# Conformer layer: four opening blocks instead of two, part of the convolution's wide sums on GpSimd, one weight group and the moments on TensorE in column groups

## The chip, the cores and the metric

The program runs on one core of one Trainium2 chip. The metric is the device time of one execution in microseconds (us); each kernel is run several times and the median is taken. The engines are called PE (TensorE: matmuls), PEld (its weight loads), DVE (VectorE), ACT (ScalarE), POOL (GpSimd) and SP (SyncE, which here only issues DMA transfers). An engine executes its own queue strictly in order; a transfer or a result of another engine is waited for by a semaphore.

## The reference

A trunk of two layers on 256 positions of width 2048, batch 1, all in float32. Every sublayer is normalised, modulated and gated by vectors computed from a conditioning vector `c` (adaLN):

```python
def causal_dwconv(u, w, b):          # depthwise, K = 31 taps
    ...
def conformer_conv(u, w_pw1, b_pw1, w_dw, b_dw, ln_g, ln_b, w_pw2, b_pw2):
    v = u @ w_pw1 + b_pw1            # 2048 -> 4096
    a, gt = jnp.split(v, 2, axis=-1)
    v = a * jax.nn.sigmoid(gt)       # GLU
    v = causal_dwconv(v, w_dw, b_dw) # 31 taps per channel
    v = jax.nn.silu(layernorm(v, ln_g, ln_b))
    return v @ w_pw2 + b_pw2         # 2048 -> 2048
def sq_relu_mlp(u, w1, w2):
    h = jax.nn.relu(u @ w1)          # 2048 -> 8192
    return (h * h) @ w2
...
mod = silu(c) @ w_mod                # per layer six vectors: shift, scale and gate, for mixer and MLP
x = x + gate * mixer(rmsnorm(x) * (1 + scale) + shift)   # layer 0: conformer, layer 1: Mamba-2
x = x + gate * mlp(rmsnorm(x) * (1 + scale) + shift)
```

The change touches only the Conformer convolution of layer 0 and the computation of `mod` that goes on beside it; the MLPs and the Mamba mixer are left as they are.

## The kernel before

Channels lie on the 128 partitions and the 256 positions in the free dimension, so the width of 2048 is 16 channel tiles ("ct"), held as 4 groups ("g") of 4.

**Product pw1 and its opening.** `native` multiplies by `w_pw1` in plain float32 (L546). The 4096 outputs are 8 blocks; a block takes 4 groups of the input (one 1 MB weight tile each) and yields the value and gate halves of two channel tiles in two PSUM banks. The first `FIRST = 2` blocks are opened together: `before(g)` computes the shift and scale of input group g, `make_u` normalises it (L471 on DVE, L474 on ACT), and both blocks multiply it before the next group is made. The other six blocks follow one by one.

**The vectors.** One job `gemv(layer, seg, ct)` streams 1 MB of `w_mod` and gives 128 numbers. Most jobs are one DVE instruction over 128x2048 with an accumulated sum (L247). The groups in `PE_GROUPS` are computed on PE instead: four matmuls with one column as the stationary side (`scol`) into one row (L236), then a copy and four tiny matmuls that turn the row into columns (L240 to L245). Jobs that nothing waits for soon are queued in `jobs`, and `pump(n)` issues n of them between other work; the `RATE` tables say how many at each step. The transfers go through one queue on SP in program order, into rings of slots called `wm` (2), `hid` (4) and `w` (3).

**The depthwise convolution.** `glu_conv` makes the gated row (L487 on ACT, L488 on DVE) into one of 4 padded rows. For each ct, ACT multiplies 24 of the 31 taps, 256 elements each (L497; 12 for the last two cts), in sets of four; DVE adds the sets as 128x1024 sums (L503), adds the other 7 taps by multiply-add (L506), folds the four partial sums (L508, L510) and subtracts a common row (L517) into the centred row `acc`. ACT squares it (L524), and POOL adds row and square to two running sums (L529, L530).

**The chain to pw2.** After the last ct, PE turns the running sums into columns (L578), DVE and ACT make mean and reciprocal deviation on 128x2 columns (L582 to L588), `spread` turns them back into rows by a diagonal matmul (L432, L433), and each ct is normalised (L596, L597), passed through silu (L598) and split in two parts for the next product (L401, L402). The product pw2 (`outer`, L300) follows; its weights are split by a cast on ACT (L292) and a subtraction on DVE (L293). All later products of the kernel are made in this way.

**Order.** The program is written in one sequence; a scheduler places each engine's instructions by priority as they become ready, `high_priority(n)` moves some ahead, and the order of SP's transfers is kept as written.

Of the kernel before, what the change touches and what calls it, by code (L numbers as in the profile page):

```python
# [8 lines left out]
F32 = mybir.dt.float32  # L9
# [6 lines left out]
P = 128  # L16
# [22 lines left out]


# [17 lines left out]
PE_GROUPS = {(0, SC2, 0), (0, SH2, 0)}  # L58
# [86 lines left out]
class Trunk:  # L145
# [40 lines left out]
    def prologue(self):  # L186
# [12 lines left out]
        for i in range(4):  # L199
# [10 lines left out]
                                compare_op=ALU.is_ge, fill=NEG, base=0, channel_multiplier=-1)  # L210
        self.eps = self.const("eps", [P, 1])
# [10 lines left out]
    def gemv(self, layer, seg, ct):  # L222

        nc = self.nc
        self.ring += 1
        tag = self.rings[self.ring % len(self.rings)]
        w = self.b(tag, [P, D], bufs=4 if tag == "hid" else 2)
        self.stream(w, self.a["wmT"][layer, seg, ct])
        g, i = divmod(ct, 4)
        m = self.mod_tile(layer, seg, g)  # L230
        if (layer, seg, g) in PE_GROUPS:
            if i == 0:
                self.row_sums = self.bank(self.ms, "ms")
            for t in range(4):
                kt = 4 * i + t
                nc.tensor.matmul(self.row_sums[:1, :], lhsT=self.scol[:, kt:kt + 1], rhs=w[:, t * 512:(t + 1) * 512],  # L236
                                 start=kt == 0, stop=kt == NT - 1)
            if i == 3:
                row = self.t("t2", [P, 512], bufs=3)[:1, :]
                nc.scalar.copy(out=row, in_=self.row_sums[:1, :])  # L240
                pc = self.bank(self.ms, "ms")
                for j in range(4):
                    nc.tensor.matmul(pc[:, j:j + 1], lhsT=row[:, j * P:(j + 1) * P], rhs=self.ones[:1, :1],
                                     start=True, stop=True)
                nc.scalar.copy(out=m, in_=pc[:, :4])  # L245
        else:
            nc.vector.scalar_tensor_tensor(out=w, in0=w, scalar=1.0, in1=self.scb, op0=ALU.mult,  # L247
                                           op1=ALU.mult, accum_out=m[:, i:i + 1])
        if i == 3:
            self.mod_done(layer, seg, g)  # L250

    def mod_done(self, layer, seg, kg):
        nc = self.nc
        m = self.mod_tile(layer, seg, kg)
        nc.gpsimd.tensor_tensor(out=m, in0=m, in1=self.col("b_mod", (layer * 6 + seg) * NT + 4 * kg, 4), op=ALU.add)  # L255
        if seg in (SC1, SC2):
            g = "norm_mix_g" if seg == SC1 else "norm_mlp_g"
            nc.gpsimd.tensor_scalar(out=m, in0=m, scalar1=1.0, scalar2=1.0, op0=ALU.add, op1=ALU.mult)
            nc.gpsimd.tensor_tensor(out=m, in0=m, in1=self.col(g, layer * NT + 4 * kg, 4), op=ALU.mult)
# [106 lines left out]
    def outer(self, srcs, make, evac, pump):  # L366

        banks = [[self.bank(self.mm, "mm") for _ in range(2)] for _ in srcs]
        for g in range(4):
            x = make(g)  # L370
            for b, src in enumerate(srcs):
                w = self.load_w(src[g])
                self.pump(pump(g))
# [22 lines left out]
    def split_x(self, dst, t, src, bias=None):  # L396
# [3 lines left out]
        if bias is None:  # L400
            nc.scalar.copy(out=hi, in_=src)  # L401
            nc.vector.tensor_tensor(out=lo, in0=src, in1=hi.bitcast(F32), op=ALU.subtract)  # L402
        else:
            nc.scalar.activation(out=hi, in_=src, func=AF.Identity, bias=bias)
            nc.vector.scalar_tensor_tensor(out=lo, in0=src, scalar=bias, in1=hi.bitcast(F32),
                                           op0=ALU.add, op1=ALU.subtract)
# [39 lines left out]
    def modulate(self, r, layer, sc, sh, g):  # L446

        ug = self.b("u", [P, 4, 2 * T], F32R)
        for t in range(4):
# [4 lines left out]
            self.split_x(ug, t, m, self.mod_tile(layer, sh, g)[:, t:t + 1])  # L454
# [3 lines left out]
    def conformer(self):  # L458
# [5 lines left out]
        r = self.rstd_bcast(ss, D)  # L464
# [3 lines left out]
        def make_u(g):  # L468
            for t in range(4):
# [7 lines left out]
        vpad = [v[:, 4 * T:5 * T + TAPS - 1] for v in room]  # L477
        for v in vpad:
            nc.gpsimd.memset(v[:, :TAPS - 1], 0.0)
        dd = [self.b("acc", [P, 4, T], bufs=5) for _ in range(4)]  # L480
        st = {"m0": None, "sum": None}

        def glu_conv(ct, bank):
            vp = vpad[ct % 4]
            v = vp[:, TAPS - 1:]
            sg = self.t("a", [P, T], bufs=3)
            nc.scalar.activation(out=sg, in_=bank[:, T:], func=AF.Sigmoid, bias=self.col("b_pw1", NT + ct))  # L487
            nc.vector.scalar_tensor_tensor(out=v, in0=bank[:, :T], scalar=self.col("b_pw1", ct),  # L488
                                           in1=sg, op0=ALU.add, op1=ALU.mult)

            taps = ACT_TAPS if ct < NT - 2 else LAST_TAPS
            wide = None
            for k in range(0, taps, 4):
                p4 = self.wp.tile([P, 4, T], F32, tag="wl" if wide is not None else "wh",
                                  name=self.nm("taps"), bufs=3)
# [4 lines left out]
                if wide is None:  # L500
                    wide = p4
                else:
                    nc.vector.tensor_add(wide, wide, p4)  # L503
            for k in range(taps, TAPS):
                o = wide[:, k % 4, :]
                nc.vector.scalar_tensor_tensor(out=o, in0=vp[:, k:k + T], scalar=self.col("w_dw", ct * TAPS + k),  # L506
                                               in1=o, op0=ALU.mult, op1=ALU.add)
            nc.vector.tensor_add(wide[:, :2, :], wide[:, :2, :], wide[:, 2:, :])  # L508
# [3 lines left out]
            if ct == 0:  # L512
                ps = self.bank(self.ms, "ms")
# [4 lines left out]
            if ct == 0:  # L518
                st["sum"] = self.t("t2", [P, 2, T], bufs=3)
                nc.scalar.activation(out=st["sum"][:, 1, :], in_=d, func=AF.Square)  # L520
                nc.vector.tensor_copy(out=st["sum"][:, 0, :], in_=d)
            else:
                sq = self.t("sq", [P, T], bufs=4)
                nc.scalar.activation(out=sq, in_=d, func=AF.Square)  # L524
                if ct == NT - 1:
                    st["last"] = d, sq
                    nc.scalar.activation(out=self.t("rcol", [P, 2])[:, :1], in_=self.eps, func=AF.Sqrt)
                else:
                    nc.gpsimd.tensor_tensor(out=st["sum"][:, 0, :], in0=st["sum"][:, 0, :], in1=d, op=ALU.add)  # L529
                    nc.gpsimd.tensor_tensor(out=st["sum"][:, 1, :], in0=st["sum"][:, 1, :], in1=sq, op=ALU.add)  # L530

        def native(blocks, rhs, done, before=None, pump=None):

            banks = {b: [self.bank(self.mm, "mm") for _ in range(2)] for b, _ in blocks}
            for g in range(4):
                if before:
                    before(g)
                ws = [self.load_w(src[g]) for _, src in blocks]
                for (b, src), w in zip(blocks, ws):
                    if pump:  # L540
                        self.pump(pump(g))
                    order = [(j, t) for t in range(4) for j in range(4)] if g == 0 else [
                        (j, t) for j in (0, 2, 1, 3) for t in range(4)]
                    for j, t in order:
                        o = banks[b][j % 2][:, (j // 2) * T:(j // 2 + 1) * T]
                        nc.tensor.matmul(o, lhsT=w[:, t, j * P:(j + 1) * P], rhs=rhs[g][:, t, :],  # L546
                                         start=g == 0 and t == 0 and j < 2, stop=g == 3 and t == 3,
                                         skip_group_check=True)
                        if g == 3 and t == 3 and j >= 2:
                            done(b, j - 2, banks[b][j - 2])  # L550

        def before(g):
            for ct in range(4 * g, 4 * g + 4):
                self.gemv(0, SC1, ct)
                self.gemv(0, SH1, ct)
            make_u(g)

        def glu(b, i, bank):
            if b == 7:
                with self.tc.high_priority(600):  # L560
                    glu_conv(2 * b + i, bank)
            else:
                glu_conv(2 * b + i, bank)

        native([(b, a["pw1"][b]) for b in range(FIRST)], u, glu, before=before)
        self.jobs += [(l, s, 4 * g + i) for l, s, g in EARLY for i in range(4)]
        rate = iter(RATE_CONF)
        pump = lambda g: next(rate)
        for b in range(FIRST, 8):
            native([(b, a["pw1"][b])], u, glu, pump=pump)  # L570
        self.pump(BETWEEN)

        ps = self.bank(self.ms, "ms")
        for i in range(4):
            q, e = divmod(i, 2)
            parts = [st["sum"][:, e, q * P:(q + 1) * P], st["last"][e][:, q * P:(q + 1) * P]]
            for k, v in enumerate(parts):
                nc.tensor.matmul(ps[:, 2 * e + q:2 * e + q + 1], lhsT=v, rhs=self.ones[:, :1],  # L578
                                 start=k == 0, stop=k == 1)
        mom = self.t("mom", [P, 6], bufs=1)  # L580
        mean, var, nmr = mom[:, 0:2], mom[:, 2:4], mom[:, 4:6]
        nc.vector.tensor_scalar_mul(out=mom[:, 0:4], in0=ps[:, 0:4], scalar1=1.0 / D)  # L582
        nc.vector.tensor_mul(nmr, mean, mean)
        nc.vector.tensor_sub(var, var, nmr)
# [473 lines left out]
```

## Time and profile before

| what | value |
|---|---|
| median of 3 runs (range) | 2636.26 us (2631.79 to 2639.38) |
| the profiled execution | 2639.67 us |
| its span on the core | 2637.9 us |
| mean granted TensorE clock | 0.983 |
| busy: PE, DVE, ACT, POOL | 2531.5, 2038.0, 1358.4, 193.1 us |
| read from memory | 652.83 MB |

The share of busy time is an average over the whole program. The stages that the change touches lie in the first 462 us: the opening, the rest of pw1 with the convolution, the chain to pw2, pw2 itself, and the start of the first MLP. The table of windows in the prediction shows each of them by itself.

### The profile page before, as it was taken

To read this page: it belongs to the slowest core of one execution; us is meant where nothing else is said; L and a number is where in the kernel's file an instruction comes from. 1 tells how busy PE (TensorE), PEld (TensorE's weight loads), DVE (VectorE), ACT (ScalarE), POOL (GpSimd) and SP (SyncE) were. 2 spreads that over 40 slices of the span, in tenths; PEclk is the share of its full clock that TensorE was granted. 3 is DMA by queue.
4 is the path that set the end of the run, shared out by engine and by line. 5 is a ranking of instruction groups with operands and counts; after the bars stand their busy time and mean duration, and the time that the engine had idled before them with its cause. 6 is when DMAs were issued, how large, how long until landed. Compare 5 with 4: busy or idle time off the path is not lost.

```text
span 2637.9 us, 36706 instructions
## 1 busy us (share of the span) xinstructions
PE 2531.5 (96%) x14359; PEld 2189.4 (83%) x14359; DVE 2038.0 (77%) x2738; ACT 1358.4 (51%) x2141; POOL 193.1 (7%) x189
## 2 busy tenths in 40 slices
PE   4799879999999999999999999999999999999998
PEld 3688469988888888898888888888997888888886
DVE  7799988987888888888877777888865565565565
ACT  2288654454443434446877766744454344443443
POOL 0023310000000000000000000000000101101000
PEclk9899889999999999999999999999999999999999
DMA  9866659788888888874655555688655555555554
GB/s 406 341 251 254 260 215 354 303 318 323 317 313 330 324 321 311 327 302 164 221 183 184 166 194 182 217 298 316 249 187 176 191 192 191 191 181 196 185 190 143
DMA packets 92591, 657.40 MB, mean 249 GB/s; under 512 B 10465, under 2 KB 10465, under 8 KB 14465
## 3 DMA queue, kind: packets, MB, share of 16 engines
q1 hardware_dynamic: 88274, 640.73, 66.3%
q0 software_dynamic: 3136, 10.59, 1.3%
q10 hardware_dynamic: 1008, 3.75, 0.4%
q8 instruction: 112, 1.84, 0.3%
q14 instruction: 61, 0.50, 0.1%
HBM read 652.83 MB, written 2.20 MB: 248 GB/s over the span
## 4 chain that ended last, share of the span: by engine, by line
PE 86%; DVE 9%; DMA 2%; issue 2%; ACT 1%; POOL 0%; ACTq 0%; SPq 0%; DVEq 0%; POOLq 0%
PE mm L300 69%; PE mm L352 4%; PE mm L351 4%; PE mm L350 4%; DVE taps L503 3%; DVE taps L506 2%; DMA hid<-wmT 2%; DVE hid L247 1%; PE mm L546 1%; DVE wm L247 1%; PE ms L972 1%; DVE wl L293 0%; PE ms L433 0%; DMA h<-xT 0%; PE ms L419 0%
## 5 line engine op out<-in xcount | busy, mean ns | idle before, releaser
L300 PE MATMUL mm<-u,wh 128*128 128x512 f32 (+1 forms) x4544 | 1378.2, 366 | 4.0 <-ACT u L401 1.9
L292 ACT CAST wh<-w 128x1024 fp32r<-128x1024 f32 x768 | 806.7, 1050 | 1027.4 <-PE mm L300 732.8
L293 DVE TENSOR_TENSOR wl<-w,wh 128x1024 fp32r<-128x1024 f32 x768 | 942.4, 1229 | 461.0 <-ACT wh L292 455.6
L300 PE MATMUL mm<-u,wl 128*128 128x256 f32 x3840 | 1083.4, 283 | 0.1
L300 PEld LDWEIGHTS mm<-u,wh 128*128 128x128 f32 x4544 | 815.3, 191 | 149.5 <-issue 3.4
L300 PEld LDWEIGHTS mm<-u,wl 128*128 128x128 f32 x3840 | 731.5, 191 | 3.8 <-issue 1.7
L300 PE MATMUL mm<-hid,wh 128*128 128x512 f32 (+1 forms) x1344 | 455.6, 389 | 2.8 <-DVE acc L644 2.8
L300 PE MATMUL mm<-hid,wl 128*128 128x256 f32 x1280 | 360.4, 282 | 0.0
L247 DVE SCALAR_TENSOR_TENSOR wm<-wm,scb 128x2048 f32<-128x2048 f32 x135 | 308.9, 2288 | 2.3 <-DMA wm<-wmT 2.3
L300 PEld LDWEIGHTS mm<-hid,wh 128*128 128x128 f32 x1344 | 249.0, 189 | 60.5 <-DVE acc L644 3.1
L546 PE MATMUL mm<-u,w 128*128 128x256 f32 x1024 | 230.2, 389 | 21.3 <-ACT u L474 21.3
L300 PEld LDWEIGHTS mm<-hid,wl 128*128 128x128 f32 x1280 | 242.6, 190 | 0.2 <-issue 0.2
L546 PEld LDWEIGHTS mm<-u,w 128*128 128x128 f32 x1024 | 199.8, 196 | 51.5 <-ACT u L474 23.0
L352 PE MATMUL mm<-wh,hid 128*128 128x512 f32 x512 | 199.9, 391 | 0.0
L350 PE MATMUL mm<-wh,hid 128*128 128x512 f32 x512 | 199.9, 390 | 0.0
L351 PE MATMUL mm<-wl,hid 128*128 128x512 f32 x512 | 199.5, 390 | 0.0
L497 ACT ACTIVATE taps<-u,par 128x256 f32<-128x256 f32 x360 | 148.6, 499 | 19.6 <-DVE u L488 10.5
L255 POOL TENSOR_TENSOR mod<-mod,par 128x4 f32<-128x4 f32 x48 | 52.5, 1094 | 1080.3 <-DVE wm L247 880.5
L247 DVE SCALAR_TENSOR_TENSOR hid<-hid,scb 128x2048 f32<-128x2048 f32 x49 | 113.9, 2329 | 14.9 <-ACT scb L202 11.2
L352 PEld LDWEIGHTS mm<-wh,hid 128*128 128x128 f32 x512 | 96.2, 188 | 19.7
L350 PEld LDWEIGHTS mm<-wh,hid 128*128 128x128 f32 x512 | 96.2, 188 | 19.7
L351 PEld LDWEIGHTS mm<-wl,hid 128*128 128x128 f32 x512 | 96.2, 188 | 19.5
(197 smaller groups left out, 1623.9 us busy)
## 6 DMA issues: line engine op xcount, KB each, us to landing
w<-w SPq DMA_DIRECT2D x256, 1024.0 KB, 4.9
wm<-wmT SPq DMA_DIRECT2D x137, 1024.0 KB, 7.2
w<-win SPq DMA_DIRECT2D x80, 1024.0 KB, 4.9
hid<-wmT SPq DMA_DIRECT2D x55, 1024.0 KB, 8.3
w<-pw SPq DMA_DIRECT2D x48, 1024.0 KB, 5.1
w<-wout SPq DMA_DIRECT2D x32, 1024.0 KB, 6.3
acc<-ac_d POOLq DMA_DIRECT2D x16, 512.0 KB, 7.2
h<-xT ACTq DMA_DIRECT2D x4, 512.0 KB, 13.1
```

Source lines behind the costliest of these rows:

```text
L247: nc.vector.scalar_tensor_tensor(out=w, in0=w, scalar=1.0, in1=self.scb, op0=ALU.mult, op1=ALU.mult, accum_out=m[:, i:i + 1])
L255: nc.gpsimd.tensor_tensor(out=m, in0=m, in1=self.col("b_mod", (layer * 6 + seg) * NT + 4 * kg, 4), op=ALU.add)
L292: nc.scalar.copy(out=wh, in_=w[:, s, :])
L293: nc.vector.tensor_tensor(out=wl, in0=w[:, s, :], in1=wh.bitcast(F32), op=ALU.subtract)
L300: mm = lambda out, lhsT, rhs, **kw: self.nc.tensor.matmul(out, lhsT=lhsT, rhs=rhs, skip_group_check=True, **kw)
L350: mm(banks[q], lhsT=hi, rhs=wh[:, k, :], start=g == 0 and t == 0, stop=False)
L351: mm(banks[q], lhsT=hi, rhs=wl[:, k, :], start=False, stop=False)
L352: mm(banks[q], lhsT=lo, rhs=wh[:, k, :], start=False, stop=g == 3 and t == 3)
L497: nc.scalar.activation(out=p4[:, q, :], in_=vp[:, k + q:k + q + T], func=AF.Identity, scale=self.col("w_dw", ct * TAPS + k + q), bias=self ...
L503: nc.vector.tensor_add(wide, wide, p4)
L506: nc.vector.scalar_tensor_tensor(out=o, in0=vp[:, k:k + T], scalar=self.col("w_dw", ct * TAPS + k), in1=o, op0=ALU.mult, op1=ALU.add)
L546: nc.tensor.matmul(o, lhsT=w[:, t, j * P:(j + 1) * P], rhs=rhs[g][:, t, :], start=g == 0 and t == 0 and j < 2, stop=g == 3 and t == 3, ski ...
```

## The change

- `FIRST` goes from 2 to 4: four blocks are open at once, in 6 banks of one PSUM pool and 2 of the other; the fourth block's weights take a `hid` slot. The last input group is made and multiplied in two halves.
- The gate vectors of the Conformer (`G1`, four groups) move from DVE to PE. A PE job now writes four rows of 32 partitions (a column group each) with the stationary column repeated 32 times.
- GLU and convolution are separated: 12 padded rows, and `conv` is written ahead of the next block's product, three cts per block.
- ACT multiplies 20 taps of every ct instead of 24 (12 for the last two), and DVE takes 11 (7 or 19). Of the wide sums, DVE keeps one (L528) and adds the side sum at the end (L534); POOL makes the other two (L527, L529), in a `hid` slot.
- The running sums on POOL go; PE sums rows and squares in four column groups of one bank (L558). The chain then works on full rows: one matmul spreads the sums (L627), the reciprocal is on 128x256, and mean and deviation are applied to four cts at a time.
- 36 jobs instead of 40 are pumped by the end of pw2, `RATE_MLP` issues 80 instead of 84, and the jobs inside the `outer` products are issued after the last split of the input.

```diff
-RATE_CONF = spread(16, 24) + spread(16, 16)
-BETWEEN = 8
+RATE_PW1 = spread(10, 16)
+BETWEEN = 10
+RATE_PW2 = spread(16, 16)
-RATE_MLP = spread(84, 116) + [0] * 50
+RATE_MLP = spread(80, 116) + [0] * 50
-FIRST = 2
+FIRST = 4
-ACT_TAPS, LAST_TAPS = 24, 12
+ACT_TAPS = 20
-PE_GROUPS = {(0, SC2, 0), (0, SH2, 0)}
+PE_GROUPS = {(0, G1, g) for g in range(4)} | {(0, SC2, 0), (0, SH2, 0)}
...
-                nc.tensor.matmul(self.row_sums[:1, :], lhsT=self.scol[:, kt:kt + 1], rhs=w[:, t * 512:(t + 1) * 512],
-                                 start=kt == 0, stop=kt == NT - 1)
+                nc.tensor.matmul(self.row_sums[32 * t:32 * t + 32, :],
+                                 lhsT=self.scol[:, kt:kt + 1].broadcast_to([P, 32]),
+                                 rhs=w[:, t * 512:(t + 1) * 512], start=i == 0, stop=i == 3, skip_group_check=True)
...
-            taps = ACT_TAPS if ct < NT - 2 else LAST_TAPS
-            for k in range(0, taps, 4):
-                ...
-                    nc.vector.tensor_add(wide, wide, p4)
-            for k in range(taps, TAPS):
+            wide = products(four("wh"), 0)
+            pair = self.b("hid", [P, 8, T])
+            aside = products(pair[:, :4, :], 4)
+            nc.gpsimd.tensor_tensor(out=aside, in0=aside, in1=products(pair[:, 4:, :], 8), op=ALU.add)
+            nc.vector.tensor_add(wide, wide, products(four("wl"), 12))
+            nc.gpsimd.tensor_tensor(out=aside, in0=aside, in1=products(four("wl"), 16), op=ALU.add)
+            for k in range(ACT_TAPS, TAPS):
                 o = wide[:, k % 4, :]
                 nc.vector.scalar_tensor_tensor(out=o, in0=vp[:, k:k + T], ...)
+            nc.vector.tensor_add(wide, wide, aside)
...
-                    nc.gpsimd.tensor_tensor(out=st["sum"][:, 0, :], in0=st["sum"][:, 0, :], in1=d, op=ALU.add)
-                    nc.gpsimd.tensor_tensor(out=st["sum"][:, 1, :], in0=st["sum"][:, 1, :], in1=sq, op=ALU.add)
+        def moments(g):
+            ...
+                    nc.tensor.matmul(st["sums"][32 * j:32 * j + 32, e * T:(e + 1) * T], lhsT=self.ones[:, :32],
+                                     rhs=st["sq"][4 * g + j][e], start=g == 0 and e == 0, stop=g == 3, ...)
...
         for b in range(FIRST, 8):
+            for _ in range(3):
+                conv(ct)
+                ct += 1
+                if ct in (8, 12):
+                    moments(ct // 4 - 2)
+            native([b], glu, pump=pump)
+        while ct < NT:
+            conv(ct)
+            ct += 1
+        moments(2)
         self.pump(BETWEEN)
...
+        with self.tc.high_priority(AHEAD_CHAIN):
+            moments(3)
+            rows = self.t("t2", [P, 2 * T], bufs=3)
+            nc.scalar.copy(out=rows, in_=st["sums"])
+            ps = self.bank(self.mm, "mm")
+            nc.tensor.matmul(ps, lhsT=self.sel, rhs=rows, start=True, stop=True)
+            ...
+            nc.scalar.activation(out=var, in_=var, func=AF.Sqrt, bias=self.eps)
+            nc.vector.reciprocal(var, var)
```

DVE in the middle of the convolution, before: one ct's own rows (`taps_1353`) with those of the next (`taps_1413`) and three jobs of `gemv` (L247) between them.

```order
L503 TENSOR_TENSOR taps_1353<-taps_1353,taps_1364 128x1024
L517 TENSOR_TENSOR acc_186<-taps_1228,ssum_529 128x256
L247 SCALAR_TENSOR_TENSOR hid_1466,mod_1301<-hid_1466,scb 128x2048
L503 TENSOR_TENSOR taps_1353<-taps_1353,taps_1370 128x1024
L247 SCALAR_TENSOR_TENSOR hid_1487,mod_1301<-hid_1487,scb 128x2048
L503 TENSOR_TENSOR taps_1353<-taps_1353,taps_1376 128x1024
L247 SCALAR_TENSOR_TENSOR wm_1527,mod_1529<-wm_1527,scb 128x2048
L503 TENSOR_TENSOR taps_1353<-taps_1353,taps_1382 128x1024
L503 TENSOR_TENSOR taps_1413<-taps_1413,taps_1418 128x1024
L506 SCALAR_TENSOR_TENSOR taps_1353<-u_178,par,taps_1353 128x256 x7
```

The same engine at the same stage, after: `hid_793` is the side sum that POOL makes.

```order
L528 TENSOR_TENSOR taps_788<-taps_788,taps_803 128x1024
L532 SCALAR_TENSOR_TENSOR taps_788<-u_184,par,taps_788 128x256 x11
L534 TENSOR_TENSOR taps_788<-taps_788,hid_793 128x1024
L535 TENSOR_TENSOR taps_788<-taps_788 128x512
L537 TENSOR_TENSOR taps_788<-taps_788 128x256
L544 TENSOR_TENSOR acc_200<-taps_788,ssum_739 128x256
```

The jobs are gone from between the rows, five wide sums became two, and DVE's last wide sum reads what POOL wrote. POOL in the convolution, before:

```order
L529 TENSOR_TENSOR t_107_532<-t_107_532,acc_184 128x256
L530 TENSOR_TENSOR t_107_532<-t_107_532,sq_591 128x256
L529 TENSOR_TENSOR t_107_532<-t_107_532,acc_184 128x256
L530 TENSOR_TENSOR t_107_532<-t_107_532,sq_651 128x256
```

and after:

```order
L527 TENSOR_TENSOR hid_749<-hid_749 128x1024
L529 TENSOR_TENSOR hid_749<-hid_749,taps_765 128x1024
L527 TENSOR_TENSOR hid_793<-hid_793 128x1024
L529 TENSOR_TENSOR hid_793<-hid_793,taps_809 128x1024
```

Two sums of 256 elements per ct became two of 1024, which DVE's L534 now waits for. ACT at the end of the convolution, after: from the last square (L547) to the copy of the summed rows (L625) that opens the chain.

```order
L547 ACTIVATE nrm_1821<-acc_203 128x256
L249 COPY t_259_1879<-ms_1856 128x512
L253 COPY mod_1855<-ms_1856 128x4
L669 ACTIVATE h_78<-h_78,gb_2846 128x256 x4
L249 COPY t_265_1913<-ms_1890 128x512
L625 COPY t_266_1931<-ms_1254 128x512
```

Two jobs' copies (L249, whose matmuls of `hid_1887` to `wm_1907` PE makes first) and four residual updates (L669) now stand between the last square and the chain, where before the last sums of POOL were waited for.

More of the change, by code (lines that the diff above doesn't have):

```diff
@@ L372, in outer @@
                 w = self.load_w(src[g])
[L373 removed]
+                with self.tc.issue_after(self.split):
+                    self.pump(pump(g))
                 with self.tc.high_priority(self.ahead if g or b else 0):
@@ L532, in native @@
-        def native(blocks, rhs, done, before=None, pump=None):
-            banks = {b: [self.bank(self.mm, "mm") for _ in range(2)] for b, _ in blocks}
-            for g in range(4):
[L536 to L565, printed above, removed]
+            tag = (("sq", 4), ("lo", 2), ("nrm", 2))[0 if ct // 4 % 2 == 0 else 1 + ct % 2]
@@ new lines, in conv @@
+            sq = self.t(tag[0], [P, T], bufs=tag[1])
+            nc.scalar.activation(out=sq, in_=d, func=AF.Square)
+            st["sq"].append((d, sq))
+            if ct == NT - 1:
+                nc.scalar.activation(out=self.t("rcol", [P, 2])[:, :1], in_=self.eps, func=AF.Sqrt)
+        def moments(g):
+            if g == 0:
+                st["sums"] = self.bank(self.ms, "ms")
+            for e in range(2):
+                for j in range(4):
+                    nc.tensor.matmul(st["sums"][32 * j:32 * j + 32, e * T:(e + 1) * T], lhsT=self.ones[:, :32],
+                                     rhs=st["sq"][4 * g + j][e], start=g == 0 and e == 0, stop=g == 3,
+                                     skip_group_check=True)
@@ L566, in conformer @@
+        native(list(range(FIRST)), glu)
+        self.rings = ("wm", "hid")
         self.jobs += [(l, s, 4 * g + i) for l, s, g in EARLY for i in range(4)]
-        rate = iter(RATE_CONF)
+        rate = iter(RATE_PW1)
         pump = lambda g: next(rate)
+        ct = 0
         for b in range(FIRST, 8):
-            native([(b, a["pw1"][b])], u, glu, pump=pump)
-        self.pump(BETWEEN)
[L573 to L579, printed above, removed]
@@ L602, in conformer, with pump @@
+        rate = iter(RATE_PW2)
+        def pump(g):
+            n = next(rate)
+            with self.tc.issue_after(last):
+                self.pump(n)
+            return 0
         st = {"ss": []}
```

176 lines of the change are left out of this document (106 added, 70 removed).

## The prediction

> **What bounds the kernel now.** I read first the windows cut at the seams of the stages. Columns: length in us; busy PE, PEld, DVE, ACT, POOL with instruction counts; granted PE clock; DMA share; GB/s.
>
> ```profile
> 0.00:42.00 42.00, 10.25 (x20) 5.19 (x20) 24.55 (x36) 13.07 (x28) 4.83 (x23) 1.00 0.97 397
> 42.00:110.00 68.00, 47.60 (x192) 39.95 (x192) 59.37 (x61) 5.79 (x13) 2.39 (x12) 0.91 1.01 421
> 110.00:130.00 20.00, 19.84 (x80) 17.03 (x81) 8.33 (x8) 14.03 (x33) 0.00 (x0) 0.86 0.45 159
> 130.00:337.00 207.00, 194.68 (x832) 150.59 (x830) 205.89 (x305) 157.99 (x386) 65.96 (x36) 0.97 0.68 256
> 337.00:359.00 22.00, 7.76 (x34) 6.65 (x35) 15.57 (x32) 7.30 (x14) 5.47 (x8) 0.58 0.26 95
> 359.00:454.00 95.00, 94.67 (x768) 94.49 (x768) 86.31 (x121) 47.57 (x70) 3.75 (x5) 0.97 0.87 331
> ```
>
> Until 110 us the transfers bound (share 0.97 and 1.01). From 130 to 337 DVE does (205.9 of 207 us), not PE, which waits there without cost. Then comes a chain of 22 us in which no engine is full, and pw2, full on PE. The change acts on these and the 8 us behind them; the other 2176 us of the span are nearly untouched. What DVE does from 130 to 337, by groups (busy, mean ns; then idle and releaser):
>
> ```profile
> L503 DVE TENSOR_TENSOR taps<-taps,taps 128x1024 f32<-128x1024 f32 x70 | 88.2, 1267 | 1.1 <-ACT taps L497 0.7
> L506 DVE SCALAR_TENSOR_TENSOR taps<-u,par,taps 128x256 f32<-128x256 f32 x136 | 58.8, 500 | 0.0
> L529 POOL TENSOR_TENSOR t<-t,acc 128x256 f32<-128x256 f32 x13 | 33.0, 2538 | 142.7 <-DVE acc L517 142.7
> L247 DVE SCALAR_TENSOR_TENSOR hid<-hid,scb 128x2048 f32<-128x2048 f32 x10 | 24.9, 2493 | 0.0
> L236 PE MATMUL ms<-hid,scol 128*1 128x512 f32 x48 | 22.8, 627 | 0.0
> L247 DVE SCALAR_TENSOR_TENSOR wm<-wm,scb 128x2048 f32<-128x2048 f32 x7 | 16.5, 2357 | 1.0 <-DMA wm<-wmT 1.0
> ```
>
> The chain of waits gives the pace, free of the overlap of a finishing instruction with the next (start, duration):
>
> ```profile
> 130.24 1.14 DVE taps L503
> 131.78 2.77 DVE taps L506 x7
> 134.54 0.40 DVE u L488
> 134.94 0.60 DVE taps L508
> 312.11 3.29 ACT taps L497 x8
> 319.37 9.50 DVE taps L506 x24
> 329.87 0.34 DVE taps L510
> 330.60 0.34 DVE acc L517
> ```
>
> So a wide sum takes 1.14 us, a multiply-add 2.77/7 = 0.396, the GLU 0.40, the first fold 0.60, an ACT tap 3.29/8 = 0.411. The small sums L510 and L517 step by 0.34. A normal ct before: 5 x 1.14 + 7 x 0.396 + 0.40 + 0.60 + 2 x 0.34 = 10.2 us; the jobs on DVE add 17 x 2.2 = 37 us in all.
>
> **What POOL costs DVE.** Decisive, because the change gives POOL four times as many elements per ct (2 x 1024 for 2 x 256), and DVE's L534 waits for them. The timeline shows POOL and DVE side by side; the first two rows are POOL's, of another stretch DVE's.
>
> ```profile
> 175.52 2.65 POOL L529 TENSOR_TENSOR t<-t,acc 128x256 f32<-128x256 f32 x1 [6.34 <-DVE acc L517]
> 178.13 1.71 POOL L530 TENSOR_TENSOR t<-t,sq 128x256 f32<-128x256 f32 x1
> ```
>
> ```profile
> 172.36 1.21 DVE L503 TENSOR_TENSOR taps<-taps,taps 128x1024 f32<-128x1024 f32 x1
> 177.51 1.74 DVE L503 TENSOR_TENSOR taps<-taps,taps 128x1024 f32<-128x1024 f32 x1
> ```
>
> The POOL sum stands from 175.52 to 178.17, nearly all of it while one job runs on DVE until 177.5; the wide sum begun at 177.51 then takes 1.74 instead of 1.21. So they take turns, and a sum of 256 costs DVE 0.53 us. Two more rows show it from the other side, and with 512 elements:
>
> ```profile
> 320.84 8.70 POOL L255 TENSOR_TENSOR mod<-mod,par 128x4 f32<-128x4 f32 x1 [9.27 <-ACT mod L245]
> 2050.20 3.54 POOL L736 TENSOR_TENSOR wm<-wm,t 128x512 f32<-128x512 f32 x2 [20.32 <-DVE t L734]
> ```
>
> ```profile
> 2050.95 1.63 DVE L293 TENSOR_TENSOR wl<-w,wh 128x1024 fp32r<-128x1024 f32 x1 [0.30 <-ACT wh L292]
> 2053.67 1.23 DVE L293 TENSOR_TENSOR wl<-w,wh 128x1024 fp32r<-128x1024 f32 x1 [1.09 <-ACT wh L292]
> ```
>
> A POOL sum of four elements lay 8.70 us behind the 24 multiply-adds that DVE issued without a gap. And L293, 1.23 us by the second DVE row, took 1.63 beside the first of two 512-wide POOL sums; the other POOL sum, done at 2050.20 + 3.54 = 2053.74, ended 1.16 us after L293 did at 2050.95 + 1.63 = 2052.58. A 512-wide sum thus holds about 1.1 us, twice the 0.53. I take 4 x 0.53 = 2.1 us for 1024; the bounds are 0 (they run side by side) and 2.65, the longest row of a POOL sum.
>
> The Trainium skill ("SBUF — State Buffer", section "SBUF: two separate sides") says the same of a DVE operation with two SBUF inputs against a POOL operation that reads SBUF: an exclusive lock, not shared bandwidth. Its "GPSIMD Engine Reference", section 3.1, gives 4497 ns for a POOL addition of 2048 elements; an estimate from that page is half, 2.25 us, and by it the sum below would be some 4 us longer.
>
> **The opening.** Four blocks are 8 MB more of weights before the last input group is complete: at 421 GB/s 20 us, so the last job's weights land near 132. PE now has 4 blocks x 128 records to do from the first input on.
>
> ```profile
> 41.94 0.52 ACT u L474
> ```
>
> ```profile
> 63.70:72.60 8.90, 8.90 (x33) 0.81 1.01 418
> 150.00:170.00 20.00, 20.00 (x94) 1.00 0.69 259
> ```
>
> At full clock a record takes 20/94 = 0.213 us, after a pause 8.9/33 = 0.27. So 512 x 0.213 + 2 for the first slow burst = 111 us from 42.5: PE runs without a pause until 153.5, later than the transfers at each group, and becomes the bound. The halves of the last group let the first bank finish after 8 of the last 64 records, at 153.5 - 13.6 + 1.7 = 141.6. On ACT follow a table load,
>
> ```profile
> 338.81 1.28 ACT L586 ACT_TABLE_LOAD   x1
> ```
>
> 16 taps and three sigmoids of GLUs, counted like taps: 1.3 + 19 x 0.411 = 9.1. DVE's first wide sum comes at 151; before, DVE was saturated from 130.2. The other four blocks need 4 x 128 x 0.213 = 109 us and end long before DVE does.
>
> **The convolution.** A ct after: 2 x 1.14 + 11 x 0.396 + 0.60 + 2 x 0.34 + 0.40 = 8.3 us on DVE, and two POOL sums of 2.1 that block it: 12.5. ACT needs 20 taps, a square and a sigmoid, 22 x 0.411 = 9.0, and is covered by that. In the first ct POOL works while DVE still waits, 4 us. So the last centred row comes at 151 + 16 x 12.5 + 1 (the first GLUs) - 4 = 348, against 336.8: **+11**. The 37 us of jobs that leave DVE, and the saved sums, are handed to POOL and come back through the turns. On PE the 16 jobs are cheap if their four column groups run together: with one column a job cost 22.8/6 = 3.8 (eight records each in the row above), in four groups about 0.95. The rows that speak for this are of the Mamba stage:
>
> ```profile
> L972 PE MATMUL ms<-acc,t 128*64 128x128 f32 x256 | 18.3, 282 | 0.0
> L961 PE MATMUL ms<-cT,t 128*128 128x128 f32 x64 | 8.4, 275 | 0.0
> ```
>
> With half the columns, two at a time, a record takes 18.3/256 = 0.071; with all of them 8.4/64 = 0.131.
>
> **The chain to pw2.** Before, POOL's last sums were late, held up by DVE, and PE's columns (L578) waited for them:
>
> ```profile
> 333.33 6.25 POOL t L529
> 341.92 2.73 PE ms L578 x12
> ```
>
> ```profile
> 357.26 1.01 PE L300 MATMUL mm<-u,wh 128*128 128x256 f32 x3 [1.93 <-ACT u L401]
> ```
>
> From 336.8 to 357.3 are 20.5 us. After, POOL's share is gone, but the copy L625 stands behind the copies of two groups of jobs, seven jobs of which PE does after the last moments. The last slots are free only when the last side sum and the first of these jobs are done, so their transfers (2.5 us each at 421 GB/s, one behind the other) end near 10 us after the last row; 12.5 to the copy and the spreading matmul. Then deviation, a table load, and a reciprocal on full rows:
>
> ```profile
> L859 DVE RECIPROCAL wm<-wm 64x256 f32<-64x256 f32 x1 | 1.7, 1744 | 0.0
> ```
>
> With silu and the split some 10 more: 22.5, **+2** (bounds -4, if the transfers are early, and +6). The cast of pw2's second weight half stands behind all 16 silus: **+1.5** (0 to 4).
>
> **The first MLP and the last.** Before, a job stood ahead of the reciprocal that opens the MLP:
>
> ```profile
> 456.18 2.29 DVE L247 SCALAR_TENSOR_TENSOR hid<-hid,scb 128x2048 f32<-128x2048 f32 x1
> 458.39 0.16 DVE L423 RECIPROCAL rcol<-rcol 128x2 f32<-128x2 f32 x1
> ```
>
> Placing jobs after the last split frees it: **-2.3** (0 to -4). Eight jobs fewer are spread; five of them now come in a bunch ahead of the last MLP's weights: 5 MB, 12 us of transfer at full rate, of which the weights loaded ahead cover most: **+3** (0 to +6). The moments on PE (32 matmuls in four groups) lie beside DVE's work and cost nothing; if PE were the bound they would cost 3 us.
>
> **Sum.** 11 + 2 + 1.5 - 2.3 + 3 = +15. On the profiled execution's 2639.7 us that is 2655; this execution stood 3.4 above the median of 2636.3, so **2652** for a median.
>
> **Rivals.** (a) POOL and DVE do overlap on 1024 elements. Then ACT's 9.0 us set the pace: 142.9 + 16 x 9.0 + 9 for the last ct = 296, 41 us sooner; with the other +4 2599. The rows of 1.21 and 1.74 speak against it; for it speaks only that no row has a sum of 1024 on POOL. It decides where a POOL sum costs DVE p with 151 + 16 x 8.3 + 30 p + 4 = 336.8, p = 1.6 us: faster below. Chance 0.14. (b) The turns cost 1.4 to 1.8 us a sum, since part of each falls on ACT's lateness or the GLU: within 0.3% (8 us, about what a measurement of this kernel can tell from no change): 2629 to 2644, chance 0.2. (c) The column groups run one after the other: seven jobs in the chain cost 2.85 us more each, +20: 2672, chance 0.06. The two rows of the Mamba stage speak against it; for it, that no row has four groups. (d) POOL starves as in the row of 8.70 us, each sum handed over 0.4 us late: 32 x 0.4 = +13, 2665; in the forecast's own range.
>
> **Chances.** Forecast 0.6 (own range 2645 to 2668), (a) 0.14, (b) 0.2, (c) 0.06. Faster 0.17 ((a) and an edge of (b)), same 0.18, slower 0.65. The range cuts most of (a), all of it below 2626, and the end of (c): 2626 to 2672.
>
> **What would show it.** In the profile after: PE without a pause from 42.5 to 153; DVE's first wide sum of the convolution (L528) near 151; the last L544 near 348; L534 waiting for POOL's L529 in most cts, POOL sums of 2.1 us and more; first pw2 product 22 us behind the last L544. If L534 hardly waits and ACT is full from 142 on, (a) is right and I am wrong. If DVE starts much before 151, my opening is wrong, and each us there is one us of the end.

## The result

| kernel | median (range), runs | ratio to before, 95% interval |
|---|---|---|
| before | 2636.32 us (2631.79 to 2639.38), 4 | |
| changed | 2696.49 us (2694.89 to 2697.7), 4 | 1.0229 (1.0212 to 1.0247) |

Slower, as forecast, but by 60 us, not by 16. The span of the profiled execution grew from 2637.9 to 2695.1. The changed kernel's windows, cut at its own seams (opening, convolution, chain, pw2, start of the MLP; columns as before):

```profile
42.00:110.00 68.00, 67.04 (x301) 58.70 (x302) 44.28 (x47) 5.45 (x12) 1.59 (x8) 1.00 0.97 398
110.00:156.00 46.00, 44.21 (x205) 38.56 (x204) 20.14 (x25) 12.12 (x28) 3.54 (x9) 1.00 0.65 250
156.00:371.00 215.00, 147.42 (x705) 112.35 (x703) 191.33 (x265) 140.03 (x348) 79.47 (x38) 0.83 0.41 151
371.00:401.00 30.00, 19.33 (x95) 6.02 (x95) 10.03 (x17) 12.22 (x22) 1.00 (x5) 0.67 0.79 322
401.00:502.00 101.00, 99.39 (x788) 94.41 (x788) 81.02 (x99) 47.36 (x73) 3.43 (x8) 0.96 0.85 324
```

The opening ends at 156 (forecast 151), the convolution takes 215 us instead of 207, and in it no engine is full any more: DVE, 99% busy before, is idle for 24 of 215 us. The chain, from the last centred row to the first pw2 product, takes 29 us instead of 20.5 (371.4 to 400.6). DVE's and POOL's groups between 156 and 371:

```profile
L532 DVE SCALAR_TENSOR_TENSOR taps<-u,par,taps 128x256 f32<-128x256 f32 x176 | 117.9, 735 | 0.5
L534 DVE TENSOR_TENSOR taps<-taps,hid 128x1024 f32<-128x1024 f32 x16 | 23.7, 1479 | 6.4 <-POOL hid L529 5.4
L528 DVE TENSOR_TENSOR taps<-taps,taps 128x1024 f32<-128x1024 f32 x16 | 21.1, 1320 | 6.4 <-ACT taps L518 6.4
L508 DVE SCALAR_TENSOR_TENSOR u<-mm,par,a 128x256 f32<-128x256 f32 x8 | 3.8, 478 | 9.5 <-ACT a L507 9.5
```

```profile
L529 POOL TENSOR_TENSOR hid<-hid,taps 128x1024 f32<-128x1024 f32 x16 | 40.2, 2513 | 35.4 <-ACT taps L518 20.7 <-DVE taps L532 14.4
L527 POOL TENSOR_TENSOR hid<-hid 128x1024 f32<-128x1024 f32 x16 | 39.3, 2456 | 95.0 <-ACT hid L518 95.0
```

The multiply-adds, 0.396 us each alone (176 x 0.396 = 70), have a busy time of 117.9. DVE's chain shows where it goes (start, duration):

```profile
183.38 8.67 DVE taps L532 x11
192.14 1.24 DVE taps L534
```

Eleven multiply-adds take 8.67 us instead of 4.36: two POOL sums lie inside them (from 184.0 and from 188.8), 2.15 us each, as the prediction had priced them. DVE's idle time has three releasers in the group rows: POOL's sum (before L534), ACT's taps (L528), and ACT's sigmoid (L508), behind which PE is late. PE, which could have run ahead, stood behind waits in its own queue:

```profile
171.39 1.19 PE L541 MATMUL mm<-taps,ones 128*128 128x256 f32 x2 [13.62 <-DVE taps L537]
237.78 1.84 PE L251 MATMUL ms<-bT,t 128*128 128x1 f32 x8 [16.02 <-ACT t L249]
309.35 1.86 PE L251 MATMUL ms<-bT,t 128*128 128x1 f32 x8 [18.23 <-ACT t L249]
```

L541 is the mean of the first tile, which waits for DVE; L251 turns a job group's row into columns and waits for a copy that stands late in ACT's queue of taps. The last GLUs came at 340 and 344 (before: 304 and 310).

### The profile page after: what moved, and what is told of

Read it like the earlier page. It is cut to its first block, busy times and chain, and to the rows that moved or that the text cites. A ratio compares the mean times of both kernels' runs of the same rounds, so it can differ in the third digit from the quotient of the medians.

```text
span 2695.1 us, 37026 instructions
## 1 busy us (share of the span) xinstructions
PE 2540.8 (94%) x14561; PEld 2194.8 (81%) x14561; DVE 2021.8 (75%) x2679; ACT 1345.7 (50%) x2112; POOL 202.4 (8%) x210
## 4 chain that ended last, share of the span: by engine, by line
PE 86%; DVE 9%; DMA 2%; ACT 1%; issue 1%; SPq 0%; POOL 0%; ACTq 0%; DVEq 0%
PE mm L312 66%; PE mm L364 4%; PE mm L363 4%; PE mm L362 4%; DVE taps L532 4%; PE mm L583 3%; DMA hid<-wmT 1%; DVE taps L534 1%; DVE wl L305 1%; DVE taps L528 1%; PE ms L1031 1%; PE ms L583 1%; DVE wm L255 1%; DMA wm<-wmT 0%; PE ms L244 0%
## 5 line engine op out<-in xcount | busy, mean ns | idle before, releaser
L305 DVE TENSOR_TENSOR wl<-w,wh 128x1024 fp32r<-128x1024 f32 x768 | 941.2, 1229 | 455.9 <-ACT wh L304 453.1
L312 PE MATMUL mm<-hid,wh 128*128 128x512 f32 (+1 forms) x1344 | 448.3, 384 | 2.5 <-DVE acc L703 2.5
L583 PE MATMUL mm<-u,w 128*128 128x256 f32 x896 | 207.6, 393 | 3.5 <-ACT u L500 3.5
L583 PEld LDWEIGHTS mm<-u,w 128*128 128x128 f32 x896 | 176.0, 198 | 38.2 <-issue 8.8
L266 POOL TENSOR_TENSOR mod<-mod,par 128x4 f32<-128x4 f32 (+1 forms) x50 | 38.3, 765 | 1235.3 <-DVE wm L255 1075.6
L532 DVE SCALAR_TENSOR_TENSOR taps<-u,par,taps 128x256 f32<-128x256 f32 x176 | 117.9, 735 | 0.5
L255 DVE SCALAR_TENSOR_TENSOR hid<-hid,scb 128x2048 f32<-128x2048 f32 x35 | 80.0, 2288 | 45.0 <-DMA hid<-wmT 33.9
```

What stands on the lines that cost most here:

```text
L305: nc.vector.tensor_tensor(out=wl, in0=w[:, s, :], in1=wh.bitcast(F32), op=ALU.subtract)
L312: mm = lambda out, lhsT, rhs, **kw: self.nc.tensor.matmul(out, lhsT=lhsT, rhs=rhs, skip_group_check=True, **kw)
L583: nc.tensor.matmul(o, lhsT=w[:, t, j * P:(j + 1) * P], rhs=u[g][:, t, :], start=g == 0 and t == 0 and j < 2, stop=g == 3 and t == 3, skip_ ...
```

## The experiments

All were timed beside the kernel before (median 2636 to 2638). "Last row" is the end of the last centred row in the profiled execution (before 337, changed 371), the point from which the chain starts.

**e1: 84 jobs again.**

```diff
-RATE_MLP = spread(80, 116) + [0] * 50
+RATE_MLP = spread(84, 116) + [0] * 50
```

> The changed kernel with RATE_MLP issuing 84 jobs again (the rest as changed), so that fewer of the five left-over G2 jobs come in one bunch ahead of the row form of the last MLP. Theory (the bunch holds up the transposes on PE, whose buffers it takes): 6 to 10 us less than the changed kernel's 2696, so 2687 to 2690. Rival (the 10 us between 1987 and 2040 come from the whole shift of the program, not from the bunch): 2696.

Measured 2689.75 us (ratio 1.0207, 1.0191 to 1.0222). The median fell by 6.7 us, the span of the profiled execution, which is the fastest of e1's four, by 10.2. SP's transfers at the start of the last MLP, changed kernel first and then e1, show the bunch and that it is gone:

```profile
2002.63 25.11 SPq L289 DMA_DIRECT2D wm<-wmT  x5
```

```profile
2003.23 0.43 SPq L289 DMA_DIRECT2D wm<-wmT  x1
```

In the changed kernel the chain ran through DVE's jobs and a transfer (`2027.42 4.81 DMA wm<-wmT`) to PE's transposes (L764); in e1 PE goes on without them. By these two executions the bunch costs 10 us, by the medians some 7; the forecast was 3.

**e2 and e3: PE not held.** e2 writes a block's product ahead of its three convolutions; e3 also turns a job's row two jobs later, into a bank of the other pool.

```diff
         for b in range(FIRST, 8):
+            native([b], glu, pump=pump)
             for _ in range(3):
                 conv(ct)
...
-            native([b], glu, pump=pump)
# e3 also, in gemv:
                 nc.scalar.copy(out=row, in_=self.row_sums)
-                for j in range(4):
-                    nc.tensor.matmul(self.row_sums[:, j:j + 1], ...)
-                nc.scalar.copy(out=m, in_=self.row_sums[:, :4])
+                self.turns.append([2, row, m, layer, seg, g])   # done at the second job from here
```

> The changed kernel with each block's product written ahead of its three convolutions, so that the mean matmul of the first row (which waits for DVE, and behind which PE stood for 13.6 us) no longer stands ahead of block 4. Theory 'PE held' (the last rows are late because PE stood behind waits on other engines): some 10 to 13 us less, 2684. Rival 'turns' (DVE and POOL taking turns set the end of the convolution by themselves): 2696, no change.

> As the run before it, and the turning of a job group's row into columns (four tiny matmuls that wait for a copy on ACT, where PE stood 16.0 and 18.2 us) is written two jobs later, into another bank. 'PE held': the last centred row comes near 350 instead of 371, 18 to 21 us less than changed, 2676. 'Turns': 2696.

Measured 2692.97 (1.022, 1.0205 to 1.0236) and 2691.56 (1.0211, 1.0195 to 1.0226): 4 and 5 us less, with intervals that overlap the changed kernel's (1.0212 to 1.0247). PE was indeed freed: the last two GLUs came at 321 and 327 (e3: 326) instead of 340 and 344. But the last row came only at 365 and 364, and 4 of these 6 to 7 us are an earlier first wide sum (152 instead of 156). In e3 DVE's last wide sum waits for POOL instead (L549 is its line there, L544 POOL's):

```profile
L549 DVE TENSOR_TENSOR taps<-taps,hid 128x1024 f32<-128x1024 f32 x16 | 27.9, 1745 | 14.8 <-POOL hid L544 14.1
```

The idle time moved from the GLU to POOL's sum. "PE held", the theory with which I began, is worth 5 us at most.

**e4: 2 jobs between convolution and chain instead of 10**, 24 in pw2 instead of 16.

> The changed kernel with 2 jobs between the convolution and the chain instead of 10, and 24 instead of 16 in pw2. Theory (PE and the copies stand behind the last weights of the jobs, which the trace shows as 8.15 us of transfer in the chain): the chain of 31.8 us shrinks by 8 to 10, of which pw2 gives back up to 4: 2688 to 2692. Rival (the chain's own vector work is as long as before, the jobs are hidden beside it): 2696 to 2700.

Measured 2699.99 (1.0247, 1.0226 to 1.0268): nothing gained. The chain from the last row to pw2 fell from 29 to 15 us, more than I had expected, but split 48 of the weights (a subtraction L305 on DVE in the first MLP, counted from 0 at pw2's first) came at 557.3, in the changed kernel at 556.2: by then all of it was paid back. The eight jobs cost as much in pw2 as in the chain.

**e5: the two POOL sums on DVE.**

```diff
-            nc.gpsimd.tensor_tensor(out=aside, in0=aside, in1=products(pair[:, 4:, :], 8), op=ALU.add)
+            nc.vector.tensor_tensor(out=aside, in0=aside, in1=products(pair[:, 4:, :], 8), op=ALU.add)
...
-            nc.gpsimd.tensor_tensor(out=aside, in0=aside, in1=products(four("wl"), 16), op=ALU.add)
+            nc.vector.tensor_tensor(out=aside, in0=aside, in1=products(four("wl"), 16), op=ALU.add)
```

> The changed kernel with its two POOL sums per channel tile back on DVE (the same additions, the same order; nothing else moves). 'Turns' (each POOL sum blocks DVE for about 2.15 us, where DVE itself needs 1.14): a tile goes from 13.2 us to 8.3 + 2 x 1.14 = 10.6, so the last centred row comes up to 16 x 2 = 32 us sooner if PE's blocks keep up, 2664; with PE's holds as they are some 15 of it, 2680. Rival (POOL's sums are hidden beside ACT's and DVE's other work, the pace is PE's): 2696 or more, since DVE then does more.

Measured 2645.79 (1.0031, 1.0021 to 1.0042): 51 of the 60 us are gone with two words. DVE does more and is done sooner:

```profile
156.00:324.00 168.00, 143.09 (x714) 108.47 (x712) 166.15 (x297) 139.90 (x349) 7.78 (x6) 0.92 0.53 196
```

```profile
L532 DVE SCALAR_TENSOR_TENSOR taps<-u,par,taps 128x256 f32<-128x256 f32 x176 | 72.7, 487 | 0.0
L529 DVE TENSOR_TENSOR hid<-hid,taps 128x1024 f32<-128x1024 f32 x16 | 19.6, 1227 | 0.0
```

DVE is full again (166 of 168 us) at 10.4 us a tile, and the last row comes at 324, 13 us before that of the kernel before, although DVE is saturated only from 156, there from 130. The multiply-adds are back at 72.7. Of the 47 us by which the last row comes sooner than in the changed kernel, 25 are busy time of DVE (191 to 166) and 22 its idle time (24 to 2). The waits on the other engines went too. In the changed kernel ACT stood at the squares of the centred rows (L547) until DVE had made the row, with the next taps and copies behind them in its queue (waits: us in total, times, longest):

```profile
ACT sq L547 <- DVE acc L544: 23.0, 6, 8.6
ACT lo L547 <- DVE acc L544: 18.7, 4, 6.8
ACT nrm L547 <- DVE acc L544: 12.5, 3, 8.2
```

These 54 us are 6 in e5, and PE's waits for the copy L249 fall from 36 to 4 us.

**e6: two opening blocks, POOL sums as changed** (and a tile convolved only once its block is there).

> The changed kernel with two opening blocks instead of four (one edit and the limits that follow from it: a tile is only convolved once its block is there). Theory (the opening costs what it delays DVE's first wide sum, 156 against 130): the first wide sum comes near 130 and the last centred row 20 to 26 us sooner, 2672. Rival (PE's holds set the pace, and with six single blocks instead of four there are more of them): 2690 to 2705.

Measured 2727.56 (1.0344, 1.0327 to 1.0361): the rival's side, and beyond it. The first wide sum came at 129 as expected, the last row at 403. With single blocks from the third on, a pair of tiles takes 32 to 44 us from 200 on; I read this as PE's holds and DVE's turns feeding each other, which no run tests by itself. Four opening blocks thus shield the changed kernel; without POOL's sums they are worth some 4 us (e8 beside e10, below).

**e7 and e8: sums on DVE, PE not held (e5 and e3 together); e8 also with two opening blocks and 84 jobs.**

> Sums on DVE, each block ahead of its convolutions, the turn of the job rows two jobs later. 'Turns': DVE now needs 10.6 us a tile and nothing holds PE, so the last centred row comes at 152 + 16 x 10.6 + 4 = 326 and the time is near 2654. 'PE held': PE's blocks, free already in the third experiment where this gave 5 us, give no more than that again: 2685.

> As the run before it, with two opening blocks and 84 jobs in RATE_MLP. Both prices then go: first wide sum near 130, last row near 130 + 16 x 10.6 + 5 = 305, chain some 27, the last MLP without its 10 us: 2636 - 32 + 7 + 5 = 2616 if DVE sets the pace; 2640 if PE's single blocks (6 x 27 us and 24 jobs) do.

Measured 2645.16 (1.0032, 1.0022 to 1.0041) and 2648.92 (1.0042, 1.003 to 1.0055). e7 is e5: with POOL out of the way PE's holds cost nothing. In e8 the first wide sum came at 127, but the last GLUs at 308 and 312 and the last row at 335: six single blocks and 24 jobs on PE take over as the bound (PE is busy for all 181 us from 127 to 308).

**e9: POOL's work without anybody waiting for it.** e5, and two POOL sums per tile on a half slot that nothing reads any more.

```diff
+            for _ in range(2):
+                nc.gpsimd.tensor_tensor(out=pair[:, 4:, :], in0=pair[:, 4:, :], in1=pair[:, 4:, :], op=ALU.add)
             for k in range(ACT_TAPS, TAPS):
```

> The kernel with the sums on DVE (e5, 2646), and on POOL two additions of 1024 elements per channel tile to a half slot whose content nothing reads any more: POOL has the same work as in the changed kernel, but DVE waits for none of its results. 'Turns' (what costs is that the two engines exclude each other on such operations): the 11 multiply-adds of a tile take 8.7 us again instead of 4.4, up to 32 x 2.1 = 67 us more, 2690 to 2712. Rival 'waits' (what costs is that DVE's last wide sum waits for POOL's result): 2646, and the multiply-adds stay at 4.4.

Measured 2693.62 (1.0218, 1.0202 to 1.0234), 48 us over e5 and 3 from the changed kernel. No row of DVE waits for POOL here, and DVE is never idle:

```profile
156.00:373.00 217.00, 151.16 (x713) 113.62 (x712) 216.73 (x297) 140.69 (x349) 119.04 (x38) 0.81 0.41 151
```

```profile
198.29 2.11 DVE L534 SCALAR_TENSOR_TENSOR taps<-u,par,taps 128x256 f32<-128x256 f32 x1
200.32 2.11 DVE L546 TENSOR_TENSOR acc<-taps,ssum 128x256 f32<-128x256 f32 x1
202.36 4.03 DVE L534 SCALAR_TENSOR_TENSOR taps<-u,par,taps 128x256 f32<-128x256 f32 x10
```

Two DVE instructions of 0.4 us take 2.11, the ten behind them their usual 0.40 each. The same DVE work took 166 us in e5 and 217 here: 51/32 = 1.6 us for each of 32 sums on which nobody waited. So a POOL sum costs DVE time even where nobody waits for it. That e9 ends within 3 us of the changed kernel is a coincidence, for in e9 DVE makes the two sums as well. In the changed kernel DVE's own work without them is 166 - 32 x 1.14 = 130 us; its 191 us then hold 62 us for the 32 POOL sums, 1.9 each, where DVE itself would need 36. These 25 us net are the price of the turns, and the 24 us of idle time come on top.

**e10 to e12: towards a better version.** e10 is e7 with 84 jobs, e11 has three opening blocks besides; e12 is e5 with three blocks and 84 jobs.

> Sums on DVE, blocks ahead of the convolutions, late turn of the job rows (e7, 2645), and 84 jobs in RATE_MLP. If the 10 us of the last MLP add to the rest as in the first experiment: 2635 to 2638, level with before. If they were covered there: 2645.

> As the run before it with three opening blocks. Theory (the opening should end when transfers and PE end together: 3 blocks give PE 3 x 27 us from 42.5 and 118 us of transfers): first wide sum near 128, DVE's 16 x 10.3 us end near 298, PE's five single blocks near 285, so the last centred row comes 25 to 30 us sooner than in e7 (329): 2610 to 2615, faster than before. Rival (as with two opening blocks in e8, PE's single blocks come too late): last row 315 to 330, 2630.

> Sums on DVE, three opening blocks and 84 jobs only, the order of blocks and convolutions and the turn of the rows as changed. If the holds on PE cost little once POOL is out of the way (e5 and e7 are equal): within 5 us of the run before it, 2612 to 2620. If they count again as soon as PE and DVE are balanced: 2625 or more.

e10 measured 2644.86 (1.0027, 1.0015 to 1.0039), e11 2649.24 (1.0047, 1.0029 to 1.0064), e12 2676.32. e12's order puts tile 14's convolution ahead of the block that makes its row, so it convolves an older row there, and its time isn't compared. e11 was a miss: the first wide sum came at 150.8, not at 128 (with four blocks, in e10, at 151.9). Its chain shows why:

```profile
95.01 23.85 PE mm L598 x96
118.88 0.33 SPq L304
120.66 11.94 DMA hid<-wmT
```

The third group's products occupy the three weight slots until 118.9; SP's queue, in order, holds the last transfers of the vectors behind the weights that wait for these slots. In the changed kernel the same pieces stand at 100 to 137. So the opening is set by slots and the order of transfers as much as by PE's work.

**e13 to e15: the column groups by themselves, in the kernel before.** e13 has the changed `gemv` with the old two PE groups, e14 adds two of the four G1 groups, e15 all four.

```diff
-PE_GROUPS = {(0, SC2, 0), (0, SH2, 0)}                                        # e13: as before
+PE_GROUPS = {(0, G1, g) for g in (1, 3)} | {(0, SC2, 0), (0, SH2, 0)}         # e14
+PE_GROUPS = {(0, G1, g) for g in range(4)} | {(0, SC2, 0), (0, SH2, 0)}       # e15
```

> The kernel before with its two PE groups of jobs computed in four column groups, nothing else. A job falls from 3.8 to 1.06 us on PE, 22 us in all between 130 and 337. If DVE alone sets the pace there, the time stays: 2634 to 2637. If PE's 195 of 207 us also count (the last GLU at 310 waits for the last block), it falls by up to 8: 2628.

> As the run before it, with two of the four G1 groups on PE too: DVE loses 8 jobs of 2.2 us (18 us), PE does 16 jobs of 1.06 (17 us) instead of 8 of 3.8 (30). Both engines are relieved between 130 and 337, so if they are the two bounds there the last centred row comes 10 to 15 us sooner: 2622 to 2627. If PE's holds at the copies of the rows count as in the changed kernel: 2636 or more.

> With all four G1 groups on PE: DVE loses 16 jobs (35 us), PE does 24 of 1.06 (25 us). PE's blocks and jobs then end near 305 and DVE's last two tiles 23 us later: 2622 to 2628 if PE is the next bound, 2605 if it is not.

Measured 2629.02 (0.9971, 0.9959 to 0.9982), 2640.55 (1.0012, 1.0003 to 1.0021) and 2642.56 (1.0022, 1.0013 to 1.0032). The column groups do what they say; PE's rows in e13, where the hid jobs took 22.8 us before:

```profile
L241 PE MATMUL ms<-hid,scol 128*32 128x512 f32 x48 | 7.6, 752 | 0.0
```

That is 1.3 us a job by the busy time, 1.0 us from one start to the next. Between 130 and 310 PE has 7 us more air, but DVE sets the pace, and the last row stays at 337. With DVE relieved of 8 or 16 jobs the last GLUs come later, at 313 and 317 instead of 310, the last row at 343 and 348: PE is then the bound, and each further job on it delays the blocks. DVE and PE were both at their limit before, within a few us. e13 is the fastest version here, faster than both kernels, but its profile shows the gain not where the edit is; see the last section.

## Why the prediction was right in sign and wrong in size

- **The price of a POOL sum** (2.1 us for 1024 elements): right. 8.67 instead of 4.36 us for the multiply-adds of a tile in the changed kernel, 1.9 us a sum over its whole convolution, 1.6 in e9. The rival that the engines overlap (a) is refuted by this. Rival (b) had a price that e9 bears out (1.4 to 1.8) and a wrong outcome: like the forecast it left out the time in which DVE is idle.
- **The convolution's sum is the step that failed** (16 tiles x 12.5 us, +11). Measured +34: the first wide sum 5 us later than forecast, DVE's busy time 191 us, about 6 less than forecast, and 24 us in which DVE is idle. The working treated DVE and POOL as one serial resource that is always fed. It is not: DVE waits for POOL's result, ACT's taps and PE's late blocks in turn, while ACT waits for DVE's rows (54 us) and PE for ACT's copies (36 us). That POOL's sums bring this loop about is shown by e5; which of its waits sets the 24 us stays open, since e3 removed one and another took its place. "On PE the 16 jobs are cheap" was right about PE's work (1.0 us each) and silent about the copy on ACT that each group of them waits for in PE's queue (16.0 and 18.2 us). Freeing PE alone gave 5 us at most, taking POOL out gave 51.
- **The opening** (PE without a pause until 153.5, first bank at 141.6, wide sum at 151): first GLU at 146.2, wide sum at 155.9. PE did run nearly without pause, but the last vectors' transfers came at 136.7, not at 132, behind weights that wait for slots. With three blocks instead of four the first wide sum comes only 1 us sooner (150.8 in e11, 151.9 in e10).
- **The chain** (+2, up to +6): +9. That the jobs' last transfers stand in it was right (`376.70 8.15 DMA wm<-wmT` in the changed kernel's chain); they end at 384.9, 14 us after the last row, not at 10. e4 shows that with two jobs instead of ten the chain is 15 us, and that the jobs cost as much in pw2.
- **pw2 and the first MLP's opening** (+1.5 and -2.3): +7 and -1.8. From the first pw2 product to the first update of the residual, 101.4 us instead of 94.8; from there to the MLP's first product, 7.5 instead of 9.3. So at the MLP's first product the program is 34 + 9 + 7 - 2 = 48 us behind. Why pw2 lost 7 no run shows.
- **The vectors of the first MLP's last input group**, which the sum put at nothing. ACT waits for the shift, whose last job on DVE ends at 568 (wait: us in total, times, longest):

```profile
ACT u L417 <- POOL mod L266: 11.9, 1, 11.9
```

  In the kernel before this wait is 1.9 us. The changed kernel is 49 us behind at split 48, 62 at split 56 and 58 at split 64. The same 11.9 us stand in every run from e1 to e11, but not in e13 to e15, which keep the old order of jobs. Between splits 48 and 64, e10 goes from 1.5 us ahead of the kernel before to 7 us behind it, so this is part of why no version built on the changed kernel gets below the kernel before. That they come from issuing 36 jobs instead of 40 by the end of pw2 is likely, but no run tests it. By split 288 the faster pace of the last section takes 11 us back, and the last MLP adds 10.
- **The last MLP** (+3, up to +6): mis-sized; 10 by the span in e1, some 7 by the medians. The bunch doesn't only delay weights, it takes the two `wm` slots that the row form of the residual needs, and PE stands behind that.
- **(c)**, the column groups one after the other: refuted by the 1.0 us a job. The starving of POOL (d) did occur in part, in the waits before L534.

## What to carry to other kernels

Where DVE is the bound, work on GpSimd over SBUF operands isn't free help: price it as DVE time (here 1.6 to 2.2 us a sum against 1.14 for the same sum on DVE), test it with dead work that nobody waits for, and expect the stall to show up on other engines, behind instructions that need DVE's result (ACT's squares here). A sum of busy times is a lower bound when the engines feed each other: look for what each waits for. When two engines are both at their limits, as DVE and PE in the kernel before, moving work from one to the other need not gain anything (e14, e15). A small result that goes from PE through another engine's long queue and back to PE can hold PE for 16 to 18 us; fetching it later freed PE here, but gave 5 us at most. And when fewer jobs are issued early, look for the first place that needs one of the later ones.

## What the runs showed that I had not expected

PE ran at two paces in the first MLP, at a granted clock of 1.00 in both. The windows of the kernel before and of e13, where the code is the same (PE alone; records in brackets):

```profile
700.00:900.00 200.00, 200.00 (x1133) 1.00 0.85 320
900.00:1100.00 200.00, 200.00 (x1133) 1.00 0.84 319
```

```profile
700.00:900.00 200.00, 200.00 (x1153) 1.00 0.86 326
900.00:1100.00 200.00, 200.00 (x1156) 1.00 0.87 329
```

PE is full in both, yet does 1133 or 1155 records in 200 us, 2% apart; over the MLP that is some 10 us, as much as e1 or e13 gained. It is not a matter of records that the profile lacks: from split 64 to split 288, counted on DVE, the kernel before takes 633 us and e13 625. The changed kernel, e5 and e7 ran at the faster pace, e10, e11, e14 and e15 at the slower, e1 changed over near 900. In the profiled executions that is why e10 shows less than e7 and e1 together: it is 5 us behind e7 at split 64 and 15 at split 288. One execution of each kernel was profiled, so differences under 10 us between the medians are uncertain in their cause. All six runs of e13 lie between 2627.4 and 2629.9, and of the 22 runs of the kernel before on the same chip one (2627.2) is as fast and the others lie from 2634.9 to 2642.4; so e13's gain is measured, but whether the column groups cause it (less work on PE ahead of the MLP) or it only goes with them stays open. No run here settles what sets the pace.
